# Modulation as one multiply-and-sum per tile along the rows, and two operand tiles moved by 128 bytes against the weight tiles

## The chip, the cores and the metric

The kernel runs on one core of one Trainium2 chip. The metric is the device time of one execution in microseconds (us), taken as the median of several runs; lower is better.

## The reference, cut to what matters

Two transformer-like blocks follow each other on 256 tokens of width 2048. The first has two layers (a gated convolution, a difference attention and a memory attention, with `w_in`, `w_mem_kv` and `w_out`). The second has one layer: a token mixer (`w_in_2`, two branch products, `w_out_2`) and a feed-forward part (`w_up_2`, a convolution, `w_down_2`). All arithmetic is in float32. The second block is modulated by one vector that depends only on the input `c_2`:

```python
c_act = jax.nn.silu(c)                       # [1, 2048]
mod = c_act @ w_mod[l] + b_mod[l]            # w_mod: [2048, 6 * 2048]
sh1, sc1, g1, sh2, sc2, g2 = jnp.split(mod, 6, axis=-1)
h = _rms_norm(x, mix_norm_pre[l]) * (1.0 + sc1[:, None]) + sh1[:, None]
```

So the modulation is a vector times a matrix of 96 MiB: little arithmetic, much to load.

## The kernel before, in words

**Products.** Every weight is read once, in pieces of 512 KB (128 partitions of 4 KB). A piece lands in one of four `raw` buffers; ScalarE copies it to float32r (`hi`), VectorE subtracts the copy (`lo = raw - hi`), and TensorE forms three products for each pair of operand and weight tile: operand-high with `hi`, operand-high with `lo`, operand-low with `hi`. Activations are kept as such a pair too: tiles `A` (high) and `B` (low), or `C` and `D`.

- Token-major products (`gemm_as`, lines 354 to 356; `gemm_halves`, lines 379 to 381): the activation tile is the stationary operand (128x128), the weight tile streams past as the moving one, 512 columns.
- Feature-major products (`gemm_ws`, lines 406 to 408): the weight tile is stationary, the activations are moving, 256 columns.

**Which tile is used where.** `xT` of the two first layers and `gv` (the input of `w_down_2`) lie in `A`, `B`; `hT` of the mixer and of the feed-forward part in `C`, `D`; `obT` (the input of `w_branch_gla_2`) in `A` and in `B` shifted by 32 floats, by the helper `pair_AB` (line 1296). In the mixer `hT` is used mostly token-major, in the feed-forward part feature-major only (20 of the 22 column chunks of `w_up_2`; the first of each half takes another operand, by `gemm_wsu`), and `gv` token-major only.

**Where tiles lie.** Tiles of a pool lie one after the other in each partition, in the order of their first use: constants, then `raw`, `hi`, `lo` (4 x 4096 bytes each), then `X16`, `C`, `D`, `A`, `B` and the rest. `C` and `D` take 16384 bytes, `A` and `B` 16 x 258 x 4 = 16512 bytes (their largest user). In the program before, `hi` starts at byte 48256, `lo` at 64640, `C` at 97408, `D` at 113792, `A` at 130176, `B` at 146688. Every one of them but `B` is a multiple of 256 bytes away from the weight tiles; `B` is 128 bytes past such a multiple, and `B` shifted by 32 floats (128 bytes) is a multiple again. The text below says *in step* for a multiple of 256 bytes and *out of step* for 128 bytes past one.

**Order of work.** `run` (line 206) walks a list of items. One queue (SP) issues all weight loads; the load of piece j+4 is issued behind the use of piece j, since it takes its `raw` buffer (RB = 4). `hi` and `lo` have four buffers each, so the splitting runs at most three pieces ahead of TensorE. Everything else (evacuations, attention heads) runs as generators that `tick` steps between items, under a budget of VectorE and ScalarE time that `Meter` estimates.

**Modulation.** `plan_mod` (line 596) makes 192 items, 24 column chunks of 512 by eight pieces; `spread_mod` (line 187) strews 64 of them over the first block, 96 over the mixer and 32 over the feed-forward part, as extra pieces in the same ring of four `raw` buffers. A piece is used by VectorE alone: two instructions `acc = raw * c + acc` of 128x512 with the activation of one input row per partition. After eight pieces `mod_done` (line 622) transposes and sums `acc` on VectorE, and after four chunks a small matmul (line 133 in the profile, as all calls that go through `Meter`) and four VectorE additions put 16 columns of the result into `modT`. Users wait by `await_tasks("mod...")`: the mixer for chunks 0 to 7, its output for 8 to 11, the feed-forward part for 12 to 19, the end for 20 to 23.

Of the kernel before, what the change touches and what calls it, by code (L numbers as in the profile page):

```python
# [11 lines left out]
ALU = mybir.AluOpType  # L12
# [48 lines left out]
    return [512] * (n // 512)  # L61


def row_tiles(n):

    return 16 if n == 16 else 1024 // n


def lay_pieces(np, name, w):

    layers, rows, n = w.shape
    out, c0 = np.empty((layers, rows * n), w.dtype), 0
    for width in cuts(name, n):
        src = w[:, :, c0:c0 + width].reshape(layers, -1, row_tiles(width), P, width).transpose(0, 1, 3, 2, 4)
        out[:, rows * c0:rows * (c0 + width)].reshape(src.shape)[:] = src
        c0 += width
    assert c0 == n
    return out
# [77 lines left out]
class Kernel:  # L156
# [306 lines left out]
    def setup(self, ctx):  # L463
        nc, tc, a = self.nc, self.tc, self.a
        pool = lambda name, **k: ctx.enter_context(tc.tile_pool(name=name, bufs=1, **k))
        self.cp = pool("consts")
        self.wp = pool("weights")
        self.ap = pool("acts")
        dp = pool("dram", space=bass.MemoryType.DRAM)
        self.scr = {n: dp.tile(s, F32, tag=n, name=n) for n, s in (  # L470
            ("x1", [2 * P, D]), ("x2", [2 * P, D]), ("x3", [2 * P, D]), ("gp1", [D]), ("gp2", [D]))}
# [12 lines left out]
        self.mhalf = self.cp.tile([P, 16], F32, tag="mhalf", name="mhalf")  # L484
        self.cols = self.cp.tile([P, 704], F32, tag="cols", name="cols")
        self.modT = self.cp.tile([P, 96], F32, tag="modT", name="modT")
        raw = self.st["xraw"] = self.ap.tile([P, 16, 256], F32, tag="X16", name="xraw")
        for k in range(2):
            self.x_load(k, 1, nc.act_dma)
        nc.vector.memset(self.mhalf, -0.5)  # L490
        self.sg = self.sm_tile("sg", [P, 6])
        self.ca = self.sm_tile("ca", [P, 16])
        nc.scalar.activation(out=self.ca, in_=self.mhalf, func=AF.Identity)
        self.warm_up()
# [15 lines left out]
    def params(self):  # L510
# [22 lines left out]

        yield
        self.st["params"] = True

    def params_attn(self):
        nc, a = self.nc, self.a
# [56 lines left out]

    def plan_mod(self):

        nc = self.nc
        self.mod_queue = deque()
        w = self.weight("w_mod_2")  # L600
        for j in range(24):
            box = {}
            for k0 in range(0, 16, 2):
                def fn(raw, j=j, k0=k0, box=box):
                    if k0 == 0:
                        if j > 1:
                            self.await_tasks(f"red{j - 2}", bg=False)
                        box["acc"] = self.cp.tile([P, 512], F32, tag="macc", name=self.nm("macc"), bufs=2)
                    acc = box["acc"]
                    for kk in range(2):  # L610
                        s = self.ca[:, k0 + kk:k0 + kk + 1]
                        if k0 + kk == 0:
                            nc.vector.tensor_scalar(out=acc, in0=raw[:, kk], scalar1=s, scalar2=None, op0=ALU.mult)
                        else:
                            nc.vector.scalar_tensor_tensor(out=acc, in0=raw[:, kk], scalar=s, in1=acc,
                                                           op0=ALU.mult, op1=ALU.add)
                    if k0 == 14:
                        self.evac.append(self.mod_done(j, acc))
                src = w.piece(k0, 2, j * 512, 512)
                self.mod_queue.append(Item("mod", fn, src, 2, 512))  # L620

    def mod_done(self, j, acc):

        nc = self.nc
        yield
        if j % 4 == 0:
            self.mred = self.cp.tile([P, 64], F32, tag="mred", name=self.nm("mred"), bufs=2)
        red = self.mred
        while not self.t1.ok():
            yield  # L630
        for h in range(2):
            tr = self.t1.get()
            nc.vector.transpose(tr, acc[:, 256 * h:256 * h + 256])
            b = 16 * (j % 4) + 8 * h
            nc.vector.tensor_reduce(out=red[:, b:b + 8], in_=tr.rearrange("p (b i) -> p b i", i=32), axis=AX.X, op=ALU.add)
            self.t1.put(tr)
        self.st[f"red{j}"] = True
        if j % 4 < 3:
            return
        yield  # L640
        yield
        pt = self.bank()
        nc.side.matmul(pt[:, 0:64], self.cst[:, C_SUM:C_SUM + P], red, start=True, stop=True)
        for q in range(4):
            b = slice(32 * q, 32 * q + 32)
            nc.vector.tensor_tensor(out=self.modT[b, 4 * j - 12:4 * j + 4],
                                    in0=pt[b, 0:64].rearrange("p (c q) -> p q c", q=4)[:, q],
                                    in1=self.cols[b, R_BMOD + 4 * j - 12:R_BMOD + 4 * j + 4], op=ALU.add)
        self.ps.put(pt)
        for i in range(4):  # L650
            self.st[f"mod{j - i}"] = True

    def mod_row(self, gcol, postcol, dst):

# [237 lines left out]
    def layer(self, l, last):  # L892
# [137 lines left out]
        def out_begin():  # L1030
# [8 lines left out]
            if last:  # L1039
                self.await_tasks(*[f"mod{j}" for j in range(8)])  # L1040
                self.shifted("G1", R_MIXPRE, 16, 0)
                st["raw"] = [self.lp.tile([P, 4, 256], F32, tag=t, name=self.nm("raw")) for t in ("dv", "dg", "mkT", "mg")]
            else:
                st["xT2"] = [self.ap.tile([P, 16, 256], F32R, tag=t, name=self.nm(t)) for t in ("A", "B")]
# [305 lines left out]
    def shift_norm(self):  # L1350
# [15 lines left out]
        self.t1.put(dg)  # L1366
        self.ps.put(pt)
        st["r_ready"] = True
        hi, lo = [self.ap.tile([P, 16, 256], F32R, tag=t, name=self.nm(t)) for t in ("C", "D")]
        st["hT"] = (hi, lo)  # L1370
        us = [raws[k // 4][:, k % 4:k % 4 + 2] for k in range(0, 16, 2)]
        for i in range(9):
# [584 lines left out]
    def open_f(self):  # L1957
# [4 lines left out]
        self.st["raw"] = [self.fp.tile([P, 4, 256], F32, tag=f"raw{n}", name=self.nm("raw")) for n in range(4)]  # L1962
        self.st["u"] = 0
        self.st["h_ready"] = self.st["r_ready"] = self.st["u_done"] = False

    def add_x(self, n, tb):

# [30 lines left out]
    def ffn(self):  # L1998
# [153 lines left out]
        for part in range(3):  # L2152
            chunks = range(4 * part, min(4 * part + 4, 11))

            def alloc():
                st["gv"] = [self.ap.tile([P, 16, 256], F32R, tag=t, name=self.nm(t)) for t in ("A", "B")]

            self.do(alloc)
            for i in chunks:
# [102 lines left out]
```

## Time and profile before

| | us |
|---|---|
| median of 3 runs | 2567.68 (2567.05 to 2570.22) |
| the profiled execution | 2563.99 |
| its span, first to last instruction | 2562.2 |
| TensorE busy | 2526.8 (99%) |
| VectorE busy | 1823.1 (71%) |
| ScalarE busy | 1266.9 (49%) |
| moved by DMA | 576.77 MB, 225 GB/s on average |

The span is from the first instruction to the last; the execution's own time is 1.8 us more. In the profile PE is TensorE's matmul, PEld its weight load, DVE VectorE, ACT ScalarE, POOL GpSimd, SP the queue that issues loads. Matmuls overlap: the shown duration of one holds its latency, and the time it really takes is the distance from its start to the next start.

### The profile page before, as it was taken

What the parts mean: (1) busy time and instruction counts of PE and PEld (TensorE: products, weight loads), DVE (VectorE), ACT (ScalarE), POOL (GpSimd) and SP (SyncE); (2) the same over time, 40 slices, a digit from 0 to 9 for tenths busy, and PEclk for the clock granted to TensorE, in tenths of its full rate; (3) what the DMA queues carried; (4) which work ended last, traced back from release to release, by engine and by line L of the source; (5) the groups of instructions that cost most, each with busy time, mean ns of one, the idle gap of its engine ahead of it and who ended that gap; (6) DMA issues with size and microseconds to landing.
All of it is one profiled execution on the core that took longest, in us unless ns stands there. A gap on an engine that the chain in (4) does not pass through costs nothing.

```text
span 2562.2 us, 38632 instructions
## 1 busy us (share of the span) xinstructions
PE 2526.8 (99%) x15079; PEld 2227.7 (87%) x15079; DVE 1823.1 (71%) x2469; ACT 1266.9 (49%) x1826; POOL 52.0 (2%) x43
## 2 busy tenths in 40 slices
PE   9999999999999999999999999999999999999998
PEld 7889998788899989878988778777999899988996
DVE  6768767786786756777777777775777667765665
ACT  6645544564554455355454334344744444543443
POOL 1000000010010000000000000000000000000000
PEclk9999999999999999999999999999999999999999
DMA  8775568887656576755558888886566766676655
GB/s 311 225 255 181 179 197 271 299 272 256 220 179 190 180 249 187 224 173 190 193 182 267 285 290 286 280 289 210 164 215 231 230 215 214 223 236 197 198 188 174
DMA packets 168903, 576.77 MB, mean 225 GB/s; under 512 B 18272, under 2 KB 24576, under 8 KB 168720
## 3 DMA queue, kind: packets, MB, share of 16 engines
q1 hardware_dynamic: 168432, 574.04, 69.0%
q8 instruction: 118, 1.93, 0.3%
q14 instruction: 65, 0.53, 0.1%
q10 hardware_dynamic: 288, 0.26, 0.0%
HBM read 565.83 MB, written 8.40 MB: 224 GB/s over the span
## 4 chain that ended last, share of the span: by engine, by line
PE 77%; DMA 9%; DVE 8%; ACT 3%; issue 2%; POOL 0%; ACTq 0%; DVEq 0%; POOLq 0%
PE acc L355 13%; PE acc L356 13%; PE acc L354 13%; PE acc L406 10%; PE acc L407 10%; PE acc L408 10%; PE pb L133 5%; DMA raw<-w_in 4%; DVE lo L133 4%; ACT hi L133 2%; DMA raw<-w_out 2%; DMA raw<-w_branch_gla 1%; DVE macc L133 1%; DMA raw<-w_branch_attn 1%; DVE tm L133 1%
## 5 line engine op out<-in xcount | busy, mean ns | idle before, releaser
L133 DVE TENSOR_TENSOR lo<-raw,hi 128x1024 fp32r<-128x1024 f32 (+1 forms) x847 | 1026.8, 1220 | 515.7 <-ACT hi L133 511.2
L133 ACT CAST hi<-raw 128x1024 fp32r<-128x1024 f32 (+1 forms) x847 | 881.7, 1048 | 867.6 <-PE acc L356 281.4
L408 PE MATMUL acc<-C,lo 128*128 128x256 f32 (+1 forms) x1424 | 403.0, 283 | 0.8 <-DVE lo L133 0.8
L406 PE MATMUL acc<-C,hi 128*128 128x256 f32 (+1 forms) x1424 | 403.7, 284 | 0.0
L407 PE MATMUL acc<-D,hi 128*128 128x256 f32 (+1 forms) x1424 | 402.9, 283 | 0.0
L354 PE MATMUL acc<-hi,C 128*128 128x512 f32 x992 | 393.1, 396 | 0.0
L355 PE MATMUL acc<-lo,C 128*128 128x512 f32 x992 | 387.4, 390 | 4.0 <-DVE lo L133 3.9
L356 PE MATMUL acc<-hi,D 128*128 128x512 f32 x992 | 387.0, 390 | 0.0
L355 PE MATMUL acc<-lo,A 128*128 128x512 f32 x904 | 357.7, 396 | 1.2 <-DVE lo L133 1.1
L356 PE MATMUL acc<-hi,B 128*128 128x512 f32 x904 | 357.9, 396 | 0.0
L354 PE MATMUL acc<-hi,A 128*128 128x512 f32 x904 | 354.2, 392 | 0.7 <-ACT hi L133 0.7
L133 DVE SCALAR_TENSOR_TENSOR macc<-raw,ca,macc 128x512 f32<-128x512 f32 x360 | 269.7, 749 | 9.9 <-DMA raw<-w_mod 2.9
L406 PEld LDWEIGHTS acc<-C,hi 128*128 128x128 f32 (+1 forms) x1424 | 271.7, 191 | 1.5 <-issue 0.7
L408 PEld LDWEIGHTS acc<-C,lo 128*128 128x128 f32 (+1 forms) x1424 | 271.7, 191 | 1.4 <-DVE lo L133 1.0
L407 PEld LDWEIGHTS acc<-D,hi 128*128 128x128 f32 (+1 forms) x1424 | 271.8, 191 | 0.6
L406 PE MATMUL acc<-A,hi 128*128 128x256 f32 x896 | 256.3, 286 | 0.0
L407 PE MATMUL acc<-B,hi 128*128 128x256 f32 x896 | 252.0, 281 | 0.0
L408 PE MATMUL acc<-A,lo 128*128 128x256 f32 x896 | 251.2, 280 | 0.3 <-DVE lo L133 0.2
L355 PEld LDWEIGHTS acc<-lo,C 128*128 128x128 f32 x992 | 186.4, 188 | 45.5 <-DVE lo L133 7.9
L354 PEld LDWEIGHTS acc<-hi,C 128*128 128x128 f32 x992 | 186.3, 188 | 40.5 <-issue 3.4
L356 PEld LDWEIGHTS acc<-hi,D 128*128 128x128 f32 x992 | 186.2, 188 | 39.3
L354 PEld LDWEIGHTS acc<-hi,A 128*128 128x128 f32 x904 | 172.7, 191 | 40.9 <-ACT hi L133 1.6
(269 smaller groups left out, 2989.5 us busy)
## 6 DMA issues: line engine op xcount, KB each, us to landing
raw<-w_in SPq DMA_DIRECT2D x406, 512.0 KB, 4.4
raw<-w_mod SPq DMA_DIRECT2D x192, 512.0 KB, 4.6
raw<-w_up SPq DMA_DIRECT2D x176, 512.0 KB, 4.2
raw<-w_out SPq DMA_DIRECT2D x96, 512.0 KB, 4.5
raw<-w_down SPq DMA_DIRECT2D x88, 512.0 KB, 4.3
raw<-w_mem_kv SPq DMA_DIRECT2D x32, 512.0 KB, 4.4
raw<-w_branch_gla SPq DMA_DIRECT2D x32, 512.0 KB, 4.7
tm<-x SPq DMA_DIRECT2D x20, 512.0 KB, 6.2
```

What stands on the lines that cost most here:

```text
L133: return f(*args, **kw)
L354: nc.tensor.matmul(o, xh[:, kt, t], hi, start=s, stop=False)
L355: nc.tensor.matmul(o, xh[:, kt, t], lo, start=False, stop=False)
L356: nc.tensor.matmul(o, xl[:, kt, t], hi, start=False, stop=e)
L406: nc.tensor.matmul(o, hi[:, c], xh, start=s and j % 2 == 0, stop=False, skip_group_check=True)
L407: nc.tensor.matmul(o, hi[:, c], xl, start=False, stop=False, skip_group_check=True)
L408: nc.tensor.matmul(o, lo[:, c], xh, start=False, stop=e, skip_group_check=True)
```

## The change

The modulation matrix is laid out anew on the host: a piece is now 128 output columns (one per partition) by 1024 input rows. The activation `c` is written to DRAM once as a row and loaded to all 128 partitions as `crow`, half of it (1024 values, 512 KB in all) at a time. A piece then takes one VectorE instruction that multiplies it by `crow` and sums along the row; the first half's sum goes to `mpart` and is the start value of the second half's, whose sum lands in `modT`. Items are ordered in three groups (columns of chunks 0 to 7, 8 to 19, 20 to 23), in each first all of one half, then all of the other, so that `crow` is loaded six times. `mod_done` with its transposes, sums and matmuls is gone. In the constants pool two `macc` (2048 bytes each) and two `mred` (256) give way to `mpart` (384) and `crow` (4096).

In the other part `D` grows by 256 bytes, and the low half of `hT` starts 128 bytes into it in the feed-forward part (`skew` 32) and at its begin in the mixer (`skew` 0); `gv` is taken from `pair_AB`, so that its low half starts 128 bytes into `B`.

```diff
+MOD_GROUPS = ((0, 8), (8, 20), (20, 24))
+def mod_order():
+    return [(h, b) for j0, j1 in MOD_GROUPS for h in range(2) for b in range(4 * j0, 4 * j1)]
...
+        self.mpart = self.cp.tile([P, 96], F32, tag="mpart", name="mpart")
+        self.crow = self.cp.tile([P, 1024], F32, tag="crow", name="crow")
...
+            def fn(raw, i=i, h=h, b=b):
+                self.await_tasks(f"crow{self.mod_half[i]}", bg=False)
+                d = raw.rearrange("p k n -> p (k n)")
+                out = self.mpart[:, b:b + 1] if h == 0 else self.modT[:, b:b + 1]
+                nc.vector.tensor_tensor_reduce(out=d, in0=d, in1=self.crow, scale=1.0,
+                                               scalar=0.0 if h == 0 else self.mpart[:, b:b + 1], op0=ALU.mult, op1=ALU.add,
+                                               accum_out=out)
+                if h and b % 4 == 3:
+                    j = b // 4
+                    nc.vector.tensor_tensor(out=self.modT[:, b - 3:b + 1], in0=self.modT[:, b - 3:b + 1],
+                                            in1=self.col(R_BMOD + b - 3, 4), op=ALU.add)
+                    self.st[f"mod{j}"] = True
+                if i + 1 < len(order) and self.mod_half[i + 1] != self.mod_half[i]:
+                    self.evac.append(self.crow_load(self.mod_half[i + 1]))
...
+    def crow_load(self, m):
+        for _ in range(2 if m else 0):
+            yield
+        h = m % 2
+        self.nc.sync.dma_start(out=self.crow, in_=self.scr["crow"][1024 * h:1024 * h + 1024].partition_broadcast(P))
+        self.st[f"crow{m}"] = True
+    def c_row(self):
+        pt = self.bank()
+        self.transpose(pt[:16, :P], self.ca)
+        row = self.t1.get([P, 256])
+        nc.vector.tensor_copy(row[:16, :P], pt[:16, :P])
+        yield
+        nc.sync.dma_start(out=self.scr["crow"].rearrange("(k p) -> k p", p=P), in_=row[:16, :P])
...
+        yield from self.crow_load(0)
...
-        hi, lo = [self.ap.tile([P, 16, 256], F32R, tag=t, name=self.nm(t)) for t in ("C", "D")]
+        hi = self.ap.tile([P, 16, 256], F32R, tag="C", name=self.nm("C"))
+        lo = self.ap.tile([P, 16 * 256 + 64], F32R, tag="D", name=self.nm("D"))
+        s = st["skew"]
+        lo = lo[:, s:s + 4096].rearrange("p (k t) -> p k t", t=256)
...
-                st["gv"] = [self.ap.tile([P, 16, 256], F32R, tag=t, name=self.nm(t)) for t in ("A", "B")]
+                st["gv"] = self.pair_AB()
```

## Rows read from the trace of the kernel before

**Rows 1.** The page: busy time and share of the span; shares of the chain by engine.
```profile
PE 2526.8 (99%) x15079; PEld 2227.7 (87%) x15079; DVE 1823.1 (71%) x2469; ACT 1266.9 (49%) x1826; POOL 52.0 (2%) x43
...
PE 77%; DMA 9%; DVE 8%; ACT 3%; issue 2%; POOL 0%; ACTq 0%; DVEq 0%; POOLq 0%
```

**Rows 2.** Busy time by stretch: feed-forward (six feature-major chunks); gates and branches of the mixer.
```profile
core 0: us, PE busy (x) PEld busy (x) DVE busy (x) ACT busy (x) POOL busy (x), PEclk, DMA share, GB/s
...
2119.70:2257.80 138.10, 138.10 (x1153) 138.10 (x1152) 99.81 (x130) 66.61 (x81) 0.00 (x0) 1.00 0.67 218
1342.60:1689.40 346.80, 338.85 (x1484) 273.25 (x1483) 271.20 (x331) 141.02 (x147) 0.70 (x1) 1.00 0.85 281
```

**Rows 3.** Line 406, first of three feature-major matmuls: feed-forward; then second layer.
```profile
engine op xcount: duration ns min/median/max, first and last start us, forms
L406 PE MATMUL acc<-C,hi x384: 283/283/283, 2119.7 to 2257.6; 128*128 128x256 f32 x192
...
L406 PE MATMUL acc<-A,hi x64: 274/282/283, 808.5 to 830.8; 128*128 128x256 f32 x64
```

**Rows 4.** Line 354, first of three token-major matmuls: w_down_2; mixer gate; w_branch_gla_2.
```profile
L354 PE MATMUL acc<-hi,A x128: 389/389/396, 1984.9 to 2073.0; 128*128 128x512 f32 x128
...
L354 PE MATMUL acc<-hi,C x32: 389/389/389, 1400.8 to 1421.9; 128*128 128x512 f32 x32
...
L354 PE MATMUL acc<-hi,A x32: 389/389/398, 1503.7 to 1524.9; 128*128 128x512 f32 x32
```

**Rows 5.** Groups by line, TensorE, w_down_2 (1985 to 2073.5 us): busy, mean ns | idle before.
```profile
L356 PE MATMUL acc<-hi,B 128*128 128x512 f32 x128 | 50.8, 397 | 0.0
L355 PE MATMUL acc<-lo,A 128*128 128x512 f32 x128 | 50.7, 396 | 0.0
```

**Rows 6.** Groups by line and shape, whole span: what VectorE does for the modulation.
```profile
L133 DVE SCALAR_TENSOR_TENSOR macc<-raw,ca,macc 128x512 f32<-128x512 f32 x360 | 269.7, 749 | 9.9 <-DMA raw<-w_mod 2.9
...
L133 DVE STREAM_TRANSPOSE t1k<-macc 128x256 f32<-128x256 f32 x48 | 20.9, 436 | 0.1
...
L133 DVE TENSOR_REDUCE mred<-t1k 128x8 f32<-128x256 f32 x48 | 20.2, 420 | 1.7
...
L133 DVE TENSOR_SCALAR macc<-raw,ca 128x512 f32<-128x512 f32 x24 | 11.5, 479 | 0.4 <-DMA raw<-w_mod 0.4
```

**Rows 7.** The same view: an accumulator read, and a VectorE product of two SBUF tiles.
```profile
L133 ACT ACTIVATION_READ_ACCUMULATOR e2k<-e2k,sm 128x1 f32 x80 | 15.2, 190 | 0.0
L133 DVE TENSOR_TENSOR tm<-tm,tm 128x512 f32<-128x512 f32 x22 | 15.1, 685 | 0.0
```

**Rows 8.** Groups by line, 1342.6 to 1689.4 us: splitting and modulation in the branch stage.
```profile
L133 DVE TENSOR_TENSOR lo<-raw,hi 128x1024 fp32r<-128x1024 f32 x120 | 146.3, 1224 | 69.9 <-ACT hi L133 69.2
L133 ACT CAST hi<-raw 128x1024 fp32r<-128x1024 f32 x119 | 125.3, 1053 | 199.6 <-DMA raw<-w_in 98.6 <-DMA raw<-w_branch_gla 44.7 <-DMA raw<-w_branch_attn 21.8
...
L133 DVE SCALAR_TENSOR_TENSOR macc<-raw,ca,macc 128x512 f32<-128x512 f32 x127 | 95.2, 750 | 3.4 <-DMA raw<-w_mod 0.9
```

**Rows 9.** The chain that ended last, 1584 to 1604 us: start us, us, what.
```profile
1588.57 1.24 DVE lo L133
...
1589.82 4.64 DMA raw<-w_branch_gla
...
1597.07 0.76 DVE macc L133
...
1598.63 4.97 DMA raw<-w_in
```

**Rows 10.** Waits of TensorE's weight loads, 1342.6 to 1689.4 us: total, times, longest.
```profile
PEld acc L355 <- DVE lo L133: 10.6, 18, 1.1
```

**Rows 11.** DMA issues: count, KB each, median us from issue to landing.
```profile
raw<-w_mod SPq DMA_DIRECT2D x192, 512.0 KB, 4.6
...
gpr<-gp SPq DMA_DIRECT2D x8, 256.0 KB, 5.7
```

**Rows 12.** Instructions on the modulation's sum tile: TensorE's part.
```profile
L133 PE MATMUL pb<-mred,cst x12: 217/273/423, 483.9 to 2324.6; 128*128 128x64 f32 x12
```

More of the change, by code (lines that the diff above doesn't have):

```diff
@@ L71, in lay_pieces @@
     layers, rows, n = w.shape
+    if name == "w_mod_2":
+        half = [w[:, 1024 * h:1024 * h + 1024, P * b:P * b + P].transpose(0, 2, 1) for h, b in mod_order()]
+        return np.stack(half, 1).reshape(layers, rows * n)
     out, c0 = np.empty((layers, rows * n), w.dtype), 0
@@ L470, in setup @@
         self.scr = {n: dp.tile(s, F32, tag=n, name=n) for n, s in (
-            ("x1", [2 * P, D]), ("x2", [2 * P, D]), ("x3", [2 * P, D]), ("gp1", [D]), ("gp2", [D]))}
+            ("x1", [2 * P, D]), ("x2", [2 * P, D]), ("x3", [2 * P, D]), ("gp1", [D]), ("gp2", [D]), ("crow", [D]))}
         self.psA = ctx.enter_context(tc.tile_pool(name="psA", bufs=2, space=bass.MemoryType.PSUM))
@@ L535, in params @@
         self.st["params"] = True
+        for _ in range(6):
+            yield
+        yield from self.c_row()
     def params_attn(self):
@@ L599, in plan_mod @@
         self.mod_queue = deque()
[L600 to L620, printed above, removed]
@@ L622, in mod_done @@
-    def mod_done(self, j, acc):
-        nc = self.nc
-        yield
[L626 to L639, printed above, removed]
+        order = mod_order()
@@ new lines, in plan_mod @@
+        for i, (h, b) in enumerate(order):
+            def fn(raw, i=i, h=h, b=b):
[12 more added lines that the diff above has]
+                    self.evac.append(self.crow_load(self.mod_half[i + 1]))
+            src = self.a["w_mod_2"][0][i * P * 1024:(i + 1) * P * 1024].rearrange("(p k n) -> p k n", p=P, k=2)
+            self.mod_queue.append(Item("mod", fn, src, 2, 512))
@@ new lines, in plan_mod @@
+        self.mod_half, m = [], -1
+        for i, (h, b) in enumerate(order):
+            m += i == 0 or h != order[i - 1][0]
+            self.mod_half.append(m)
+    def crow_load(self, m):
[5 more added lines that the diff above has]
+    def c_row(self):
+        nc = self.nc
+        pt = self.bank()
+        self.transpose(pt[:16, :P], self.ca)
+        row = self.t1.get([P, 256])
+        nc.vector.tensor_copy(row[:16, :P], pt[:16, :P])
+        self.ps.put(pt)
+        yield
+        nc.sync.dma_start(out=self.scr["crow"].rearrange("(k p) -> k p", p=P), in_=row[:16, :P])
+        self.t1.put(row)
@@ L640, in mod_done @@
         yield
         yield
[L642 to L648, printed above, removed]
@@ L649, in mod_done @@
-        self.ps.put(pt)
-        for i in range(4):
-            self.st[f"mod{j - i}"] = True
+        yield from self.crow_load(0)
     def mod_row(self, gcol, postcol, dst):
@@ L1041, in out_begin @@
                 self.shifted("G1", R_MIXPRE, 16, 0)
+                st["skew"] = 0
                 st["raw"] = [self.lp.tile([P, 4, 256], F32, tag=t, name=self.nm("raw")) for t in ("dv", "dg", "mkT", "mg")]
@@ L1964, in open_f @@
         self.st["h_ready"] = self.st["r_ready"] = self.st["u_done"] = False
+        self.st["skew"] = 32
     def add_x(self, n, tb):
```

## The prediction

> **What bounds the kernel now.** I read the page first: TensorE is busy 99% of the span, VectorE 71%, ScalarE 49%, and the chain that ended last runs through TensorE for 77% [rows 1]. So time comes from two places only: from how long a matmul really takes, and from the few stretches where TensorE waits. Busy time by stretch tells where those are. In the feed-forward part TensorE has no hole and VectorE is at 99.8 of 138.1 us; in the gate and branch stage of the mixer TensorE is busy 338.9 of 346.8 us, with VectorE at 271.2 and the DMA engines at 85% [rows 2]. That stage also holds some 68 of the 192 modulation pieces: 127 of the two-operand instructions [rows 8], which are 15 of the 16 that eight pieces need (127 x 16 / 15 / 2).
>
> For the true length of a matmul I take, from the view by line, first and last start of the first of three matmuls and divide by the number of threes between. Feature-major: in the feed-forward part (2257.6 - 2119.7) / 383 = 360.0 ns per three, in the second layer (830.8 - 808.5) / 63 = 354.0 ns [rows 3]. Token-major: `w_down_2` (2073.0 - 1984.9) / 127 = 693.7 ns, a mixer gate 680.6 ns, `w_branch_gla_2` (1524.9 - 1503.7) / 31 = 683.9 ns [rows 4]. Shapes and counts per piece are equal; what differs is where the low tile lies. Out of step (128 bytes past a multiple of 256 from the weights) are `B` in the layers and in `w_down_2`; in step are `D`, and `B` in `w_branch_gla_2`. So feature-major products are slower in step, token-major ones slower out of step; there, the two instructions on either side of the load of `B` last 396 and 397 ns [rows 5] instead of 389 [rows 4].
>
> **The change part by part.** *Feature-major, `D` moved out of step.* 20 chunks x 16 row tiles x 4 column tiles = 1280 threes, 360.0 - 354.0 = 6.0 ns each: 7.7 us. The starts are rounded to 0.1 us, which over 63 threes is 1.6 ns: 5.6 to 9.8 us. No other work hides or eats this: TensorE is the bound there, and VectorE and ScalarE are below three quarters [rows 2], so what is late next still has slack.
>
> *Token-major, `B` put in step for `w_down_2`.* 44 row tiles x 2 token blocks x 4 chunks = 352 threes, 693.7 - 680.6 = 13.1 ns: 4.6 us; by the slower in-step row (683.9) 3.4 us. Together 12.3 us, bounds 9.0 to 14.4. Nothing else leaves its step: the constants pool shrinks by 128 bytes, which moves weights and operands alike, and `D` grows by 256, a multiple. `xT` stays out of step in its token-major products, and `skew` 0 keeps the mixer's `hT` where it was.
>
> [...]
>
> *The modulation on VectorE.* Now: 269.7 + 11.5 + 20.9 + 20.2 = 322.3 us [rows 6], 1.68 us per piece. Then: one instruction of 128x1024 per piece, whose price the trace does not show. Below it lies the subtraction of two SBUF tiles of that shape, 1.224 us [rows 8]; with an accumulator read as ScalarE pays it, 0.19 us [rows 7], 1.41 us. I take 1.3, between these two. The upper end is a row of half speed: from 512 to 1024 columns the two-operand product goes from 0.685 [rows 7] to 1.224, so 1.05 ns a column and 0.15 fixed; at 2.1 ns a column and with the read, 2.5 us. At 1.3 us VectorE does 72 us less over the kernel and 68 x 0.38 = 26 us less in the branch stage. Nearly all of this is off the path. It counts only where TensorE waits.
>
> *What the relief is worth.* In the branch stage 480 threes at 0.681 us are 326.7 us; the stage takes 346.8. The other 44 matmuls (1484 - 1440, transposes and sums) last 0.27 us each if they are like the sums [rows 12], overlapped with their neighbours: 0 to 12 us, and I take 5. That leaves 15 us of waiting, of which the profile names 10.6 in 18 waits for `lo` [rows 10]. The stage goes at the pace of the four `raw` buffers: 188 pieces (120 splits and 68 of the modulation) are 47 turns of 7.4 us, and a turn on the chain is a load of 4.6 to 5.0, a cast of 1.05 and a subtraction of 1.22 us, or a load and two instructions of 0.76 [rows 8, 9]. A turn holds 1.45 modulation pieces, so VectorE gets 0.55 us less work in each, but the load stays. ScalarE sits idle for 199.6 us there, mostly for loads [rows 8]. I take 5 of the 15 us, bounds 0 and 13.
>
> *What goes on TensorE.* Six small sums, 12 records of 0.27 us [rows 12], mostly overlapped: 1 us, bounds 0.8 and 3.3. The additions into `modT` stay 24 in number and cost no more.
>
> *What is added.* Once: a transpose, a copy and an 8 KB write, then a read; this stands in an early chunk, 20 pieces or so before the first use, with three split pieces and four landed ones before TensorE. SP waits for the copy, its later loads with it, but no sooner than the ring would let them go: 0.3 us, bounds 0 and 1. Six times: `crow` is loaded, 512 KB on SP's queue, which also waits there until VectorE has used the old half, with the next weight loads behind it. They wait for the same piece anyway. A broadcast of half the size takes 5.7 us to land, a plain piece of the full size 4.6 [rows 11]; I bound it by 4.6 and 11.4. The next modulation instruction waits for it on VectorE, and the subtractions behind it wait too. Three of the six fall where no modulation piece is near (before the first, and between the groups). In the middle of the first block and of the feed-forward part three split pieces, 8 us of TensorE work, cover a wait of that size; without cover they cost up to 3 us each. The fourth half falls behind the 48th of the mixer's 96 pieces, in the branch stage, where there is no lead: 11.4 less two pieces at 1.8 us, up to 8 us, at least 0. I take 2 us, near the 1 us that the plain piece's landing would leave.
>
> **Sum.** 12.3 + 5 + 1 - 0.3 - 2 = 16 us. The profiled execution took 2563.99 us (span 2562.2 and 1.8 around it) and would take 2548; the median of the runs is 3.7 us above the profiled one, so I forecast 2552 us. All best ends together give 31 us less (2537), all worst ends, without the half-speed instruction, 5 us more (2573). The case's own range is 2544 to 2560.
>
> **Rivals.**
> *The relief is worth nothing.* The ring is paced by loads, and the waits of TensorE stay: 12.3 + 1 - 2.3 = 11, 2557 us. For it: the idle ScalarE waiting for loads; against: subtraction and modulation stand on the chain between the loads [rows 9]. Chance 0.17.
>
> *The step does nothing.* The difference in rows 3 and 4 comes from the stage and not from the address (other neighbours, other weights). Then 5 + 1 - 2.3 = 4 us: 2564 us, no change that can be told. Against it: `w_branch_gla_2` has `A` and `B` too and runs at the in-step rate [rows 4]. Chance 0.07.
>
> *`crow` waits three times in full.* 8 + 3 + 3 us take the gain down to some 3 or 4: 2564 us. For it: the broadcast's 5.7 us for half the bytes. Chance 0.06.
>
> *The multiply-and-sum runs at half speed.* This is the slower side: 2.5 us per piece. In the branch stage 68 x 0.81 = 55 us more VectorE work, 326 of 346.8 us; each turn gets 1.2 us longer, and with half of that on the chain 47 turns lose 28 us. 12.3 + 1 - 2.3 - 28 = -17: 2585 us. It decides from about 2.0 us per instruction, where 47 x 1.45 x 0.5 x 0.32 = 11 eats the rest. Against it: the old instruction, also with two float32 SBUF inputs, takes 0.749 us for 512 columns [rows 6], not twice 0.685. Chance 0.11.
>
> [...]
>
> **How the numbers follow.** The forecast has 0.57, the rivals 0.17, 0.07, 0.06 and 0.11, and 0.02 is left. Measured times of this kernel tell about 0.2% (5.1 us), so faster means below 2562.6, slower above 2572.8. Faster: 0.57 + 0.17 and about a third of the two cases at 2564, 0.78. Slower: 0.11 and 0.02, 0.13. Within: 0.09. For 8 in 10 the range reaches from near the sum of the best ends to past the two cases at 2564: 2539 to 2566. The likeliest case's own is above.
>
> **What would show it.** In the feed-forward part the threes of line 406 at 354 ns and in `w_down_2` at 681 ns, with lines 355 and 356 at 389; if they stay, the step does nothing. The new instruction's mean: 1.2 to 1.45 us for me, above 2.0 for the slower rival; VectorE's busy time down to about 1750 us. In the branch stage TensorE's waits for `lo` below 10.6 us, or not; and a wait of VectorE for the load of `crow` around 1470 us, of some 2 us for me, near 8 for the third rival. I would be wrong if the address effect held for one of the two kinds of product alone, or if another operand lost its step.

## The result and the profile after

The kernel after takes 2547.83 us, median of 4 runs (2546.72 to 2548.51), beside 2567.36 us for the kernel before (4 runs, 2564.64 to 2570.22): ratio 0.9923, 95% interval 0.9906 to 0.9941. That is 19.5 us less where 16 were forecast (2552). A second comparison on another chip gave 2549.35 beside 2564.82 us, 15.5 less (`after_again` below), so the gain is known to some 4 us only. One of the five runs of `step_only` below took 3547 us at a granted clock of 0.65 and is in no ratio. The profiled execution took 2548.07 us, span 2546.3, so the two traces compared below differ by 15.9 us. The forecast is near in the sum by luck: two of its terms were wrong by some 8 us each, in opposite directions.

The page after, to be read against [rows 1]: busy time, then shares of the chain.
```profile
PE 2509.8 (99%) x15068; PEld 2218.0 (87%) x15068; DVE 1749.5 (69%) x2374; ACT 1265.4 (50%) x1826; POOL 53.6 (2%) x43
...
PE 76%; DMA 10%; DVE 8%; ACT 4%; issue 2%; ACTq 0%; POOL 0%; DVEq 0%; POOLq 0%; SPq 0%
```
TensorE is 17.0 us shorter and VectorE 73.6 us. In the chain the DMA engines and ScalarE each have a per cent more and TensorE one less.

The same two stretches as in [rows 2], found by the same matmuls:
```profile
2111.66:2247.10 135.44, 135.44 (x1152) 135.44 (x1151) 96.98 (x128) 66.55 (x81) 0.00 (x0) 1.00 0.68 223
1350.26:1692.48 342.22, 336.20 (x1480) 275.31 (x1479) 246.70 (x300) 140.87 (x147) 0.69 (x1) 1.00 0.86 287
```
The feed-forward stretch lost 2.66 us with the same work in it. The branch stage lost 4.6 us of span and 24.5 us of VectorE.

First of three feature-major matmuls in the feed-forward part [rows 3] and first of three token-major ones in `w_down_2` [rows 4], by line:
```profile
L418 PE MATMUL acc<-C,hi x384: 274/282/283, 2111.7 to 2247.0; 128*128 128x256 f32 x192
...
L366 PE MATMUL acc<-hi,A x128: 389/389/398, 1979.4 to 2065.8; 128*128 128x512 f32 x128
```
And by groups, the two beside the load of `B` in `w_down_2` [rows 5]:
```profile
L367 PE MATMUL acc<-lo,A 128*128 128x512 f32 x128 | 49.8, 389 | 0.0
L368 PE MATMUL acc<-hi,B 128*128 128x512 f32 x127 | 49.4, 389 | 0.0
```
A three (the three matmuls of one pair of tiles) takes (2247.0 - 2111.7) / 383 = 353.3 ns instead of 360.0, and (2065.8 - 1979.4) / 127 = 680.3 ns instead of 693.7.

The modulation on VectorE, which answers to [rows 6] (groups: busy, mean ns, idle before):
```profile
L145 DVE CUSTOM_DVE_ANT_0 raw<-raw,crow,mpart 128x1024 f32<-128x1024 f32 x96 | 122.8, 1280 | 17.5 <-DMA crow<-crow 12.6 <-DMA raw<-w_mod 4.4
L145 DVE CUSTOM_DVE_ANT_0 raw<-raw,crow 128x1024 f32<-128x1024 f32 x96 | 116.9, 1218 | 6.1 <-DMA raw<-w_mod 6.1
...
L145 DVE DVE_READ_ACCUMULATOR2_ANT mpart<- 128x1 f32 x96 | 7.9, 83 | 0.0
```
The new instruction runs at the pace of the subtraction of the same shape [rows 8], and its read of the accumulator takes 0.08 us: 1.33 us per piece instead of 1.68. The 12.6 us of idle time for `crow` stand in two waits. In the branch stage TensorE's weight loads now wait as follows [rows 10]:
```profile
PEld acc L367 <- DVE lo L145: 7.1, 4, 4.6
```
There were 18 short waits; now there are 4, and one of 4.6 us holds most of it.

Where the time went, worked out from the starts of the 14,064 large matmuls, which are the same and in the same order in all these kernels. Each row is the difference to the profiled execution of the kernel before, in us, by stage (its times in the head); the last column is the whole span. The later kernels are explained below.
```
             0-417  417-511  511-1343  1343-1753  1753-1852  1852-2562   span
after         +2.2    +6.6     -1.1       -9.2       -1.6      -12.8    -15.9
after_again   +0.6    +5.7     -1.2       -5.0       -1.6      -12.8    -14.2
step_only     +0.1    +1.1     +0.0       +1.3       -1.2      -12.8    -11.5
mod_only      +0.4    +8.9     -1.1       -4.6       -1.6       -0.1     +1.8
crow_once     +0.7    -0.6     -0.9      -11.5       -1.6      -14.3    -28.2
pad_dve       +2.0    +1.5     +0.4       -7.4       +0.0      -13.1    -16.6
full_row      +0.9    -0.3     +3.2      -11.6       -1.2      -13.6    -22.8
two_tiles     +2.0    -1.3     -1.2      -10.3       -1.6      -12.7    -25.0
crow_early    +1.1    +0.7     -0.6       -9.4       +0.0      -14.0    -22.3
gap           +5.7    +1.2     +0.4      -15.3       -0.8      -13.6    -22.5
mixer_skew    +1.9    +5.1     +0.8       -8.2       -1.5      -12.8    -14.7
both_skew     +0.2    +5.3     -1.5       -5.1       -1.5       -7.1     -9.7
skew_64       +1.6    +6.2     -0.7       -5.1       -1.1      -12.8    -11.8
```
The last stage repeats within 0.1 us in six of the kernels with the step and gains up to 1.5 us more in the others. The branch stage (1343 to 1753) differs by 4 us between two executions of one kernel (`after`, `after_again`), so no single number of it is to be trusted to less. Each row is one execution.

### The profile page after: what moved, and what is told of

Read it like the earlier page. It is cut to its first block, busy times and chain, and to the rows that moved or that the text cites. A ratio compares the mean times of both kernels' runs of the same rounds, so it can differ in the third digit from the quotient of the medians.

```text
span 2546.3 us, 38548 instructions
## 1 busy us (share of the span) xinstructions
PE 2509.8 (99%) x15068; PEld 2218.0 (87%) x15068; DVE 1749.5 (69%) x2374; ACT 1265.4 (50%) x1826; POOL 53.6 (2%) x43
## 3 DMA queue, kind: packets, MB, share of 16 engines
HBM read 568.98 MB, written 8.41 MB: 227 GB/s over the span
## 4 chain that ended last, share of the span: by engine, by line
PE 76%; DMA 10%; DVE 8%; ACT 4%; issue 2%; ACTq 0%; POOL 0%; DVEq 0%; POOLq 0%; SPq 0%
PE acc L368 12%; PE acc L367 12%; PE acc L366 12%; PE acc L419 10%; PE acc L418 10%; PE acc L420 10%; PE pb L145 5%; DVE lo L145 4%; DMA raw<-w_in 4%; DMA raw<-w_out 3%; ACT hi L145 3%; DMA raw<-w_branch_gla 2%; DVE raw L145 1%; DMA raw<-w_mod 1%; DVE tm L145 1%
## 5 line engine op out<-in xcount | busy, mean ns | idle before, releaser
L419 PEld LDWEIGHTS acc<-D,hi 128*128 128x128 f32 (+1 forms) x1424 | 266.3, 187 | 0.6
L367 PEld LDWEIGHTS acc<-lo,A 128*128 128x128 f32 x904 | 170.5, 189 | 43.5 <-DVE lo L145 7.3
```

The source lines that it names most:

```text
L367: nc.tensor.matmul(o, xh[:, kt, t], lo, start=False, stop=False)
L419: nc.tensor.matmul(o, hi[:, c], xl, start=False, stop=False, skip_group_check=True)
```

## The experiments

**The two parts alone.** `step_only` is the kernel before with these lines of the change (and those that set `skew`), and `bufs=1` for `mred`:
```diff
+        lo = self.ap.tile([P, 16 * 256 + 64], F32R, tag="D", name=self.nm("D"))
+        lo = lo[:, s:s + 4096].rearrange("p (k t) -> p k t", t=256)
...
-                st["gv"] = [self.ap.tile([P, 16, 256], F32R, tag=t, name=self.nm(t)) for t in ("A", "B")]
+                st["gv"] = self.pair_AB()
```


> The kernel before with the step of the operand tiles alone (D out of step in the feed-forward part, B in step for w_down_2); the modulation stays as it was. To make room for the longer D, the small sums' tile has one buffer instead of two. Theory: the step is worth its 1280 x 6.0 + 352 x 13.1 ns, so 12.3 us: 2555 us, threes of the feed-forward products at 354 ns and of w_down_2 at 681 ns. Rival 1, the threes got shorter because VectorE does less beside them: no step in the threes here, 2567 us. Rival 2, part of the changed kernel's gain in these stages came from fewer waits: the threes move as said but the whole gives under 8 us.

`mod_only` is the kernel after with those taken back:
```diff
-        self.st["skew"] = 32
+        self.st["skew"] = 0
...
-                st["gv"] = self.pair_AB()
+                st["gv"] = [self.ap.tile([P, 16, 256], F32R, tag=t, name=self.nm(t)) for t in ("A", "B")]
```


> The kernel after without the step: skew 0 in the feed-forward part, A and B plain for w_down_2; the modulation as multiply-and-sum with its crow loads stays. Theory: what is left of the gain is 19.6 - 12.3 = 7 us, so 2560 us, with the first layers some 8 us longer than before and the branch stage some 9 us shorter. If the two parts help each other, more of the gain goes: 2563 us or above. If the step is worth nothing, it stays at 2548 us.

Measured on one chip beside the kernel before (2564.89 us): `step_only` 2551.61 us, ratio 0.9948 (0.9934 to 0.9961), 13.3 us less; `mod_only` 2561.59 us, ratio 0.9993 (0.9984 to 1.0002), no change that can be told. Groups of `w_down_2` in `step_only`, and first of three in the feed-forward part of `mod_only`:
```profile
L355 PE MATMUL acc<-lo,A 128*128 128x512 f32 x127 | 49.4, 389 | 0.0
L356 PE MATMUL acc<-hi,B 128*128 128x512 f32 x127 | 49.4, 389 | 0.0
```
```profile
L418 PE MATMUL acc<-C,hi x389: 283/283/283, 2119.9 to 2259.6; 128*128 128x256 f32 x195
```
The step alone gives the threes of the kernel after; without it they are the 360 ns of before ((2259.6 - 2119.9) / 388), under the same modulation. So the step is worth its 12.8 us of the last stage wherever the rest stands, and the rival that the stage and not the address sets a three is dead. The modulation as it stands is worth 3.3 us by the medians, with an interval from 4 us to nothing, and not the 7 that I expected.

**Which step.** Three kernels move the operand tiles otherwise. `both_skew` moves `C` as well (`mpart` of 48 columns and 12 small slots make room):
```diff
+        hi = self.ap.tile([P, 16 * 256 + 64], F32R, tag="C", name=self.nm("C"))
...
-        lo = lo[:, s:s + 4096].rearrange("p (k t) -> p k t", t=256)
+        hi, lo = [v[:, s:s + 4096].rearrange("p (k t) -> p k t", t=256) for v in (hi, lo)]
```


> The kernel after with C moved by 128 bytes as well in the feed-forward part, so that both operand tiles of the feature-major products are out of step with the weights (mpart 48 columns and 12 small slots, to make room). Theory (a product is slow when its moving operand lies in step with the weights): now one of three products has a moving operand out of step and a three takes 6.7 ns less; with all three out of step it takes 13 to 20 ns less than the 360, 8 to 17 us below the kernel after, 2531 to 2540 us. Rival 1, what counts is that the two operand tiles differ from one another: back to 360 ns per three, 8 us above the kernel after, 2556 us. Rival 2, one tile out of step already breaks the pattern and the second adds nothing: 2548 us.

`skew_64` moves `D` by 16 columns (64 bytes) and not by 32:
```diff
-        self.st["skew"] = 32
+        self.st["skew"] = 16
```


> The kernel after with D moved by 64 bytes and not by 128 in the feed-forward part. If any other step will do: 2548 us, with the threes of the feature-major products at 353 ns. If it must be half of 256 bytes: 360 ns, 8.5 us above the kernel after, 2556 us.

`mixer_skew` moves `D` in the mixer as well, where most products are token-major:
```diff
-                st["skew"] = 0
+                st["skew"] = 32
```


> The kernel after with D out of step in the mixer too, where its products are mostly token-major. Theory: by the address rule 19 token-major chunks of 32 threes lose 13.1 ns each, 8.0 us, and 128 feature-major threes gain 6.7 ns, 0.9 us: 7 us longer than the kernel after, 2555 us, and the mixer's threes at 694 ns, in the same stages, with the same work beside them. Rival: the difference belongs to the stage: no change, 2548 us. If the ring's waits in the branch stage hide it, 2550 us.

Measured: `both_skew` 2555.91 us, ratio 0.9968 (0.9956 to 0.9981); `skew_64` 2547.17 us, 0.9936 (0.9922 to 0.9949); `mixer_skew` 2549.23 us, 0.9942 (0.9929 to 0.9954). Feed-forward groups of `both_skew`; the first of three there by line, and in the first six chunks of the last stage; the same as the former in `skew_64`; and groups of a mixer gate (1409 to 1431 us) in `mixer_skew`:
```profile
L420 PE MATMUL acc<-C,lo 128*128 128x256 f32 x384 | 109.4, 285 | 0.0
L419 PE MATMUL acc<-D,hi 128*128 128x256 f32 x384 | 109.1, 284 | 0.0
L418 PE MATMUL acc<-C,hi 128*128 128x256 f32 x384 | 107.9, 281 | 0.0
```
```profile
L418 PE MATMUL acc<-C,hi x384: 281/281/281, 2113.9 to 2251.8; 128*128 128x256 f32 x192
...
L418 PE MATMUL acc<-C,hi x352: 279/281/285, 1853.0 to 1977.9; 128*128 128x256 f32 x176
```
```profile
L418 PE MATMUL acc<-C,hi x384: 278/278/278, 2115.7 to 2251.1; 128*128 128x256 f32 x192
```
```profile
L366 PE MATMUL acc<-hi,C 128*128 128x512 f32 x32 | 12.4, 389 | 0.0
L368 PE MATMUL acc<-hi,D 128*128 128x512 f32 x31 | 12.3, 397 | 0.0
L367 PE MATMUL acc<-lo,C 128*128 128x512 f32 x31 | 12.3, 396 | 0.0
```
With both tiles out of step the threes of this stretch are back at (2251.8 - 2113.9) / 383 = 360.1 ns, and the kernel loses 7 to 8 us by the medians, as rival 1 said. So the theory that each moving operand must leave the weights' step falls: two thirds of the gain need the high and the low operand tile to differ from one another. That is not the whole rule. In the first six chunks of the last stage, and in its last three, the same kernel's threes take (1977.9 - 1853.0) / 351 = 356 ns, between the two rates, so that this stage loses 5.8 us to the kernel after and not 8.6; why is open. Of the two distances tried, 64 bytes do as well as 128: a three takes (2251.1 - 2115.7) / 383 = 353.5 ns beside 353.3.

In the mixer the address rule holds instruction by instruction (396 and 397 instead of 389 ns, in the same stage with the same neighbours; the starts of that gate's threes are 693.5 ns apart instead of 680.6), but its price does not arrive: by the table 1.9 us more than in the kernel after from 511 to 1343 us and nothing that can be told behind it, where I had reckoned 7. It may be that a slower matmul only shortens a wait where TensorE waits for the ring; that is argued and not shown. In the feed-forward part TensorE waits for nothing (busy 135.44 of 135.44 us in the kernel after), and there the step pays in full: 6.7 ns in each three.

**What the relief and the loads of `crow` are worth.** `crow_once` loads `crow` once:
```diff
         h = m % 2
-        self.nc.sync.dma_start(out=self.crow, ...)
+        if m == 0:
+            self.nc.sync.dma_start(out=self.crow, ...)
```


> The kernel after, but crow is loaded once and never again, so the second half of each sum uses the first half's values of c (the modulation's second halves are left out in that sense). All other instructions stay. Theory: two of the five later loads stop TensorE (in the first block at 491 us, 4.7 us, and in the attention branch at 1475 us, 5.3 us): 10 us shorter than the kernel after, 2538 us, and no wait of VectorE for crow. Rival 1, these holes have another cause (the order of the side work): under 2 us. Rival 2, the loads also cost in the feed-forward part by taking the queue: 13 us or more.

`pad_dve` is that with VectorE's time put back:
```diff
                                                accum_out=out)
+                nc.vector._e.tensor_scalar(out=d[:, :256], in0=d[:, :256], scalar1=1.0, scalar2=None, op0=ALU.mult)
```


> The kernel with crow loaded once (second halves use the first half's values of c), with one more VectorE instruction behind each multiply-and-sum, a product by 1.0 in place over 128x256 of the piece, which nobody reads. By the 512 and 1024 column rows it takes about 0.4 us, so a piece costs VectorE again the 1.7 us it did before; the order of all other instructions stays. Theory: the relief of the branch stage is VectorE's time per piece: its 11 us come back, 2548 us. Rival 1, the relief comes from the sums that left TensorE and from another order of the side work: 2538 us. Rival 2, the ring is paced by loads: 2538 us too, with VectorE's idle time shorter.

Measured: `crow_once` 2537.72 us, ratio 0.9900 (0.9887 to 0.9914); `pad_dve` 2546.34 us, 0.9928 (0.9915 to 0.9940). The group of the added instruction in `pad_dve`, and the waits of TensorE's weight loads for `lo` in the branch stage, there and then in `crow_once`:
```profile
L627 DVE TENSOR_SCALAR raw<-raw 128x256 f32<-128x256 f32 x192 | 56.5, 294 | 6.6
```
```profile
PEld acc L367 <- DVE lo L145: 6.6, 13, 1.1
```
```profile
PEld acc L367 <- DVE lo L145: 4.7, 7, 1.1
```
Without the later loads the kernel is 10 to 12 us shorter than the kernel after (2547.83 and 2549.35 us), as expected, and the stage from 417 to 511 us shows 7.2 of them (6.6 + 0.6). VectorE's time is on the path, though it is busy 69%: 56.5 us of added work cost 8.6 us by the medians and 11.6 by the profiles, 15 to 21% of it; 1.2 of the 11.6 stand in the last stage, where the threes differ (see the end). That settles it against "paced by loads alone". It does not settle all of the branch stage's gain: some 70 pieces with 0.29 us put back lose 4.1 us there, no more than two executions of one kernel differ by, where 70 with 0.35 us taken away had gained 11.5. At least 2 us of the 11.5 are a wait for one of the sums that left TensorE (shown in the part on the prediction). What the rest is (another order of the side work, the 4 us between two executions) stays open.

**Why a load of 512 KB costs 5 us.** VectorE in the kernel after, first block (start us, us, what, idle before), and SP's queue at the same time:
```profile
487.93 1.23 DVE L145 TENSOR_TENSOR lo<-raw,hi 128x1024 fp32r<-128x1024 f32 x1 [1.20 <-ACT hi L145]
495.51 1.28 DVE L145 CUSTOM_DVE_ANT_0 raw<-raw,crow,mpart 128x1024 f32<-128x1024 f32 x1 [6.35 <-DMA crow<-crow]
...
496.72 2.36 DVE L145 TENSOR_TENSOR lo<-raw,hi 128x1024 fp32r<-128x1024 f32 x2
```
```profile
484.74 4.77 SPq L234 DMA_DIRECT2D raw<-w_in  x3
489.57 0.43 SPq L646 DMA_DIRECT2D crow<-crow  x1
```
The load of the second half stands on SP's queue behind three weight loads, and those wait for their own buffers until 489.5 us. Only then is it issued, 6.0 us after VectorE's last use of the old half (482.36 + 1.22), and 5.9 us later VectorE goes on. The next modulation instruction is already due, so VectorE stands still for 6.35 us with two subtractions behind it, and TensorE runs out of split pieces. The chain shows the order, down to the subtraction that frees the third load's buffer; below it TensorE's wait, and the stretch behind the wait (us, busy time of each engine, granted clock, DMA share, GB/s):
```profile
487.93 1.24 DVE lo L145
489.17 0.02 issue
489.19 0.33 SPq L234
...
489.57 5.83 DMA crow<-crow
...
496.81 1.15 DVE lo L145
```
```profile
498.00 0.75 PE L367 MATMUL acc<-lo,A 128*128 128x512 f32 x1 [3.92 <-DVE lo L145]
```
```profile
498.00:501.52 3.52, 3.52 (x8) 2.77 (x9) 3.52 (x4) 0.00 (x0) 0.00 (x0) 0.52 0.82 261
```
TensorE stands still for 3.9 us, and then pays again. Its granted clock, 1.00 before, is 0.52 over the next 3.52 us: eight matmuls start 0.43 us apart and not 0.23, 1.7 us more. The hole in the attention branch is of the same kind (4.2 us of standing, then eight starts in 3.5 us at a granted clock of 0.51). So some 5.6 and 5.9 us are lost at the two places, before what later waits make up. Four kernels take this apart. `crow_early` issues the load right behind the last use of the old half:
```diff
-        for _ in range(2 if m else 0):
+        if False:
             yield
```


> The kernel after with the later crow loads issued right behind the last use of the old half, and not two pieces later. Theory: the hole in the first block comes from SP's order, since the load stands behind three weight loads that wait for their buffers from 484.7 to 489.5 us, and the next modulation instruction is due at 489.2; issued at 484.8 it lands near 490.6 and VectorE waits 1.5 us there instead of 6.35, and 4 instead of 6.26 us in the attention branch, 1.5 to 2 us sooner: 5 to 7 us below the kernel after, 2542 us. Rival: what costs is the transfer's 5.8 us itself, in the way of the weights wherever it stands: 2547 us.

`gap` does that too, and `spread_mod` leaves one place empty at each change of half (`mpart` has 48 columns):
```diff
-        step, have = sum(dens) / n_mod, 0.0
+        step, have = sum(dens) / (n_mod + 1), 0.0
...
+                k = len(self.mod_half) - len(self.mod_queue)
+                if n_mod and self.mod_half[k] != self.mod_half[k - 1]:
+                    have -= step
```


> As the early loads, and at each change of the half one place of the spread modulation pieces is left empty (the others move closer by a part in 33 or 97), so that some 10 us lie between the last use of the old half and the first of the new one in the attention branch. Theory: no modulation instruction waits for c any more; what is left is the transfer in the branch stage, which cost the version with two tiles 2.5 us there: 2540 us, level with two tiles. Rival: pieces that stand closer press on VectorE elsewhere: 2544 us or above.

`full_row` keeps all of c in `crow`:
```diff
-        self.crow = self.cp.tile([P, 1024], F32, tag="crow", name="crow")
+        self.crow = self.cp.tile([P, 2048], F32, tag="crow", name="crow")
...
-                nc.vector.tensor_tensor_reduce(out=d, in0=d, in1=self.crow, scale=1.0,
+                nc.vector.tensor_tensor_reduce(out=d, in0=d, in1=self.crow[:, 1024 * h:1024 * h + 1024], scale=1.0,
...
-            self.e2 = Slots(self.gp, "e2k", 4, 512)
+            self.e2 = Slots(self.gp, "e2k", 2, 512)
```


> The kernel after with both halves of c kept side by side in crow (2048 columns, loaded once); the 4 KB that this takes come from the mixer's e2k slots in the gate and attention stage, 2 instead of 4. Theory: as with crow loaded once, 10 us shorter than the kernel after, 2538 us, if two e2k slots are enough for the sliding-window attention and the gated linear attention; if those stages go at the pace of the slots, some us come back between 1000 and 1340 us, and the whole is 2538 to 2548 us. Rival: the holes are not the loads', 2548 us or above.

`two_tiles` keeps the first half in `crow` and the second in a tile of each phase's pool:
```diff
+    def new_crow1(self, pool):
+        self.crow1, self.st["crow1"] = pool.tile([P, 1024], F32, tag="crow1", name=self.nm("crow1")), False
...
+            self.new_crow1(self.mp)
+            self.evac.append(self.crow_load(1))
```


> The kernel after with the two halves of c in two tiles: the first half in crow, loaded once; the second in a tile of whichever phase pool is open (first layers, branch stage, feed-forward part), loaded at the start of each, long before it is used. The e2k slots stay 4. Theory: no modulation instruction waits for c, and nothing is lost in the gated linear attention: 4.5 us (the profiles' difference at 1330 us) below the full row's 2541, so 2537 us, as with crow loaded once. Rival: the three loads still take 5.5 us of the ring each when they come; if TensorE has no cover there, 2541 us or above.

And the kernel after once more, beside `crow_early`, `gap` and `skew_64`:

> The kernel after, beside the two mends of the crow loads: all theories expect 2548 us, and the holes at 491 and 1475 us again.

Measured: `crow_early` 2542.70 us, ratio 0.9919 (0.9903 to 0.9934); `gap` 2542.93 us, 0.9923 (0.9908 to 0.9937); `full_row` 2541.12 us, 0.9908 (0.9893 to 0.9923); `two_tiles` 2540.50 us, 0.9911 (0.9895 to 0.9926); `after_again` 2549.35 us, 0.9941 (0.9928 to 0.9954). In `crow_early`, VectorE at the same place and at its second wait, in the attention branch; and SP's queue at both:
```profile
488.82 1.29 DVE L145 CUSTOM_DVE_ANT_0 raw<-raw,crow,mpart 128x1024 f32<-128x1024 f32 x1 [3.53 <-DMA crow<-crow]
...
1476.30 1.28 DVE L145 CUSTOM_DVE_ANT_0 raw<-raw,crow,mpart 128x1024 f32<-128x1024 f32 x1 [6.26 <-DMA crow<-crow]
```
```profile
481.34 0.43 SPq L646 DMA_DIRECT2D crow<-crow  x1
482.76 2.89 SPq L234 DMA_DIRECT2D raw<-w_in  x2
...
1470.07 0.33 SPq L234 DMA_DIRECT2D raw<-w_mod  x1
1470.45 0.42 SPq L646 DMA_DIRECT2D crow<-crow  x1
```
The early load wins the first block by SP's order alone (+0.7 us in that stage instead of +5.7 and +6.6), with the same transfer, so it is the order and not the transfer that costs there. VectorE's wait fell to 3.53 us, not to my 1.5, since the load now took 7.3 us to land instead of 5.8; of that TensorE's split pieces covered all but 0.7 us, and its granted clock stayed at 1.00. In the branch stage nothing moved, contrary to my 1.5 to 2 us: 6.26 us again. There the load is behind the weight loads in either kernel, and the first piece of the new half follows at once. The empty place of `gap` is what helps there (-15.3 us, the best of all in that stage, where VectorE's one wait for `crow` is now 2.7 us). But it loses 4.6 us more than `crow_early` in the first layers, where its pieces stand closer (one trace each), so in the sum it is no better.

`full_row` and `two_tiles` wait for `crow` nowhere. `full_row` gives back 4 us from 511 to 1343 us, where two `e2k` slots seem too few (TensorE has a wait of 3.6 us for ScalarE there that `crow_once` has not); `two_tiles` doesn't, but is level with it and not 4 us ahead, as I expected. Its load in the branch stage, issued at 1418 us, can be a part of that: the 192 matmuls that begin at 1423 us before take 47.0 us in it, 44.5 in the kernel after and 45.5 in `crow_once`, which is 1.5 us and not the 2.5 that I had put on it; the rest stays open. Both beat the two kernels of this case: their runs (2538.29 to 2541.31 and 2539.01 to 2542.59 us) lie below all nine runs of the kernel after (2545.04 to 2550.09). By the ratios they are clear of `after_again` and not of the first comparison (0.9906 to 0.9941); `crow_early`'s and `gap`'s intervals overlap both. `crow_early` with the empty place in the mixer alone was not tried.

## Why the prediction was right, point by point

*Step of the operand tiles, 12.3 us: right.* 6.7 and 13.4 ns per three instead of 6.0 and 13.1, so 1280 x 6.7 + 352 x 13.4 = 13.3 us. `step_only` measures 13.3 by the medians (its interval reaches from 10 to 17) and 12.8 in the last stage of its trace. The rows at 0.1 us sufficed because 31 threes and more stood between first and last. That the addresses do nothing, as one rival has it, has `step_only` and `mod_only` against it by 13 us. `both_skew` shows that two thirds of the feed-forward part's gain hang on how the two operand tiles lie to each other.

*Price of the new instruction, 1.3 us: right.* 1.218 and 1.280 us and 0.08 of read; VectorE's total fell by 73.6 us (72 forecast) and in the branch stage by 24.5 (26 forecast). By the sums of durations the modulation itself fell from 322.3 to 255.5 us, 66.8 less, so the nearness of 73.6 and 72 is in part chance. The slower rival is dead. Its 2.1 ns a column was my estimate, twice the 1.05 of the plain product, and no run shows a multiply-and-sum at that speed: with two float32 sources in SBUF and an accumulator that is read, the new instruction takes 1.218 and 1.280 us beside the subtraction's 1.224.

*Relief, 5 us, and the six sums, 1 us: right in kind, 8 us too small together.* With the later loads of `crow` out of the way the kernel is 13.9 us shorter than `step_only` by the medians of one chip (2551.61 and 2537.72 us), and by its profile 28.2 us shorter than before, 14.3 of them in the last stage, where the step is. What is left, 13.9 us, is put down to the relief and the sums; 11.5 of it lie between 1343 and 1753 us. I had looked at the stage up to 1689.4 us only. Behind it, in `w_out_2`, one of the six sums held TensorE up in the kernel before; its wait, and the stretch behind it:
```profile
PE pb L133 <- DVE mred L133: 3.3, 1, 3.3
```
```profile
1716.42:1719.46 3.04, 3.04 (x8) 2.37 (x9) 2.26 (x6) 0.84 (x1) 0.00 (x0) 0.53 1.02 392
```
I had priced a sum by its own 0.27 us and not by the wait for its operand, nor by the clock of 0.53 behind that wait. The 96 matmuls that begin at 1702.5 us take 28.9 us in the traces of the two kernels that keep the sums (`before`, `step_only`) and 24.9 to 26.6 in the twelve traces without them. `pad_dve`, which puts back VectorE's time but no sum, takes 26.6, so 2 us and more here are the sums' and not the relief's. And I had taken a third of the waits because the ring is paced by loads; yet `pad_dve` shows that in a ring of four buffers VectorE's time counts with the load's: 56.5 us put back cost 8.6.

*`crow`, 2.3 us and 0.3 for the row: wrong, 8 us too small.* The later loads cost 12.3 us by the profiles of `after` and `crow_once`, 1.5 of them in the last stage, where no wait for `crow` stands: some 10.8 us, and 10 to 12 by the medians (six chunks that run at 350 ns per three in `crow_once` make most of those 1.5). The step that failed is "In the middle of the first block and of the feed-forward part three split pieces, 8 us of TensorE work, cover a wait of that size". In the feed-forward part the cover was not needed: 18.8 us lie there between the two modulation instructions, and the load had landed. In the first block the next one is due after 6.8 us, and the cover did not hold. I had counted the landing from VectorE's last use, and the load is issued 6.0 us later, behind weight loads which themselves wait; it lands 11.8 us after that use, above my upper bound of 11.4. When VectorE stopped, TensorE had 4.9 us of split work left and not 8 (489.2 to 494.1 us). And no term held the slow clock behind a hole, 1.7 us each time. "They wait for the same piece anyway" was said of the loads behind `crow`; I had not asked the same of the loads ahead of it. In the branch stage the wait came much as the third rival had it, 6.26 us on VectorE where it said near 8; TensorE's chunk there is 5.5 us longer than in `crow_once`, and the next one made up 2.1 of it.

So of the rivals, the one that puts the relief at nothing is refuted by `crow_once` and `pad_dve`, the one on the step by `mod_only`, half speed by the groups. The one on `crow` was right that the waits come in full at the two places where VectorE stands, and wrong on the third, in the feed-forward part; for its 2564 us it would have needed the relief to be as small as I took it. So the forecast of 2552 us came near by luck: 8 us too little for the relief and the sums, 8 us too little for `crow`.

## What to carry to other kernels

A forecast can be near because two errors cancel; only runs that take one term out at a time show it. When a step adds a DMA, look at what stands *ahead* of it on its queue and when that may go, not only at its own landing time and at what is behind. A small instruction that waited for its operand cost the engine 3.3 us here, and not its own 0.27, and holes of 3.3 to 4.2 us on TensorE were paid a second time at a granted clock of 0.51 to 0.53. When TensorE takes two operand tiles in turn and waits for nothing, compare the first and last start of long rows of equal matmuls over the addresses of the tiles: 6.7 and 13.4 ns each were half a per cent in sum here (13 us), while 13 ns on most threes of the mixer came to 1.9 us where I had reckoned 7.

## What the runs showed of the hardware

- Feature-major threes (128x256, float32, stationary weights) take 360.0 ns when both moving tiles lie in the weights' step. With both 128 bytes out they take 360.1 in one stretch and 356 in another (`both_skew`), and with only the low one out, by 128 or by 64 bytes, 353.3 to 353.5. Token-major threes (128x512) go the other way: 680.3 ns in step, 693.7 with the low stationary tile 128 bytes out; both tiles out was not tried for them. Why is open. So is why in some executions with these very relative addresses some chunks run at 350.0 ns per three: the six from 1852 us on in `crow_once` and `crow_early`, the last three in `full_row` and `gap` (0.21 us less per 192 matmuls).
- After holes of 3.9 and 4.2 us (kernel after) and 3.3 us (kernel before) TensorE's granted clock was 0.51 to 0.53 over the next 3.0 to 3.5 us, and matmuls started 0.43 us apart instead of 0.23. After a hole of 0.7 us (`crow_early`, 490.6 us) and one of 0.8 us (kernel before, 455.8 us) it stayed at 1.00.
- The multiply-and-sum of 128x1024 float32 from SBUF takes 1.218 us, with its start value read from a tile 1.280, beside 1.224 for a plain subtraction of that shape; the read of the accumulator takes 0.08 more.
- Half of the row `crow` (4 KB) spread over 128 partitions (512 KB written) lands after 5.2 to 7.4 us in the six loads of the kernel after, the middle ones 5.7 and 5.8, beside a median of 4.6 for a plain piece of the same size (`w_mod`). The profile counts 568.98 MB read from HBM instead of 565.83; the 3.15 MB between them are six times 512 KB, so each partition's copy counts as a read of its own.
